# A two-layer hybrid trunk on one core: the tail's products held in traced order on TensorE, and all modulation of the next layer moved beside the tail

## The chip, the cores and the metric

The kernel runs on one core of one Trainium2 chip. The metric is the time of one execution in device microseconds; several executions are timed, and their median is given. TensorE multiplies (PE, with its weight loads as PEld), VectorE (DVE), ScalarE (ACT) and GpSimd (POOL) do the rest, and SyncE (SP) issues the transfers.

## The reference, cut to what matters

Two layers (`DEPTH = 2`), each over 1152 tokens of 1024 channels: 128 context and 1024 latent tokens.

```
def modulation(cvec, mod_w, mod_b):
    m = jax.nn.silu(cvec) @ mod_w + mod_b              # 1024 x 3072, for c and for c_ctx
    return jnp.split(m.reshape(-1, 1, 3 * D_MODEL), 3, axis=-1)
...
    shift, scale, gate = mod
    h = rmsnorm(x, norm_g) * (1 + scale) + shift
    return split_cols(h @ w_in), gate
...
    xb = centred_conv(x_b, P['conv_w'], P['conv_b'])
    ob, st = rglru_bidir(xb, h0, P)                    # gates: two block products per direction
...
    m = jax.nn.sigmoid(merge).reshape(B, T, N_BRANCH, D_MODEL)
    y = (m[:, :, 0] * ((oa * jax.nn.silu(g_a)) @ P['w_br_a'])
         + m[:, :, 1] * ((ob * jax.nn.silu(g_b)) @ P['w_br_b'])
         + m[:, :, 2] * ((oc * jax.nn.silu(g_c)) @ P['w_br_c']))
    return x + gate * (y @ P['w_out'])
```

`merge` is the last 3072 columns of `h @ w_in`. Every product is of float32 operands, cut into a high and a low part and multiplied in three matmuls.

## The kernel before, in words

A layer has three parts. `unit_phase` does the projections and the two attentions. The **tail** does the merge gates and the three branch products. `w_out_phase` does the last projection, in two halves `q` of 512 columns, each 9 token blocks of 24 matmuls of 128x512.

The tail is written as 22 calls of `tail_step` and one of `tail_last`, which has the last two column blocks of branch B. A step has one block of 128 output channels of one branch, in three chunks of 384 tokens. For a chunk, `tail_merge` runs 24 matmuls (`ws_chunk`, over weights `wsh` and `wsl` that are loaded and split for this step) into a PSUM tile `ps_s`, and ACT's Tanh (L1022) takes it to `mg`. `tail_branch` runs 12 matmuls (`oh`, `ol` against `wb`) into `ps_s` or `ps_o`, one chunk later than its merge (three later in two steps), and VectorE multiplies by the gate and adds to `yr`.

Beside the tail runs a generator, `L.rec`, which `tail_step` moves on by one piece a chunk. It first holds the recurrence of branch B, four column blocks of `lru`: the transfer `lx`, one ACT operation into `lu` (L860), nine DVE operations of the convolution on `lu`, the split of `lu` into `luhl` (ACT for the high half, POOL for the low), then 12 groups of three gate matmuls `ps_t<-luhl,gw`, and the scans. Behind these it holds `mod_side`, the **modulation**: pieces of up to 384 columns of `mod_w`, each 1024 rows long, loaded in three parts `modw` (3, 3 and 2 blocks of 128 rows) through two buffers. For each row block and each of two condition vectors one DVE operation multiplies a block into the accumulator `macc` (16 operations a piece). Six matmuls with a column of ones, the **sums** (L957; the hardware runs each in two passes), then add over partitions into `ps_t`, and DVE writes `modt` from it.

Layer 1 has 11 pieces: the three of its own gate, and eight of layer 2. `NMOD = 8` of them run in the tail, the other three in the first half of `w_out_phase`. Layer 2 has none.

A scheduler orders each engine's instructions from its own estimate of durations and from priorities; the order of the program is a wish, data dependencies bind. Tiles come from rings of buffers; a new tile waits until the last reader of the one it replaces is done. The ring `tab` has one buffer, `D` three, `T` two.

Of the kernel before, what the change touches and what calls it, by code (L numbers as in the profile page):

```python
# [2 lines left out]

# [1 line left out]

# [14 lines left out]
NTOK = 1152  # L20
# [6 lines left out]
TPO = 1500  # L27
# [3 lines left out]
NLAG = 3  # L31

LRU0 = 4
NMOD = 8

WUK = 1
XPOS = 1
# [16 lines left out]
def hybrid_dit_kernel(ctx, tc, I, O):  # L54
# [28 lines left out]
    V, A, Pq, T = nc.vector, nc.scalar, nc.gpsimd, nc.tensor  # L83
# [20 lines left out]
    one = tl("one", 1)  # L104
# [61 lines left out]
    def w_in_cols(l, c0):  # L166
        def f(lo):
            dma(lo, I["w_in"][l, :, c0:c0 + 128].rearrange("(k p) n -> p k n", p=128))
        return f

    def mm3(out, lh, ll, rh, rl, first, last):
        T.matmul(out=out, lhsT=r(lh), rhs=r(rh), start=first, stop=False)  # L172
        T.matmul(out=out, lhsT=r(lh), rhs=r(rl), start=False, stop=False)  # L173
        T.matmul(out=out, lhsT=r(ll), rhs=r(rh), start=False, stop=last)  # L174

    class Lay:
        pass
# [662 lines left out]
    def lru(L, ct):  # L840

        l, D = L.l, L.D
# [18 lines left out]
        uhl = {}  # L861
# [15 lines left out]
        for c in range(3):  # L877
            s = slice(384 * c, 384 * c + 384)
            for d in range(2):
                for k, (dst, hb) in enumerate(((ra, D.hba), (ri, D.hbx))):  # L880
                    p = ps("t", 384)
                    m = 2 * k + d
                    mm3(p, wh[:, m, :], wl[:, m, :], uhl[c][:, 0, :], uhl[c][:, 1, :], True, True)
                    A.activation(out=dst[d][:, s], in_=p, func=AF.Tanh, scale=0.5,
                                 bias=hb[:, 4 * d + ct:4 * d + ct + 1])
            if c == 0:
                parts(2)
            yield
            for d in range(2):
                stt(ri[d][:, s], ri[d][:, s], 1.0, u[:, s], ALU.add, ALU.mult)  # L890
# [49 lines left out]
            load_o(L, 1, (k,))  # L940
            yield

    def mod_side(mods, tag, atag):

        seq = [(m, k0, min(k0 + 3, KT)) for m in mods for k0 in range(0, KT, 3)]
        ws = {}

        def load(i):
            (D, b0, n), k0, k1 = seq[i]
            ws[i] = al(tag, "modw", k1 - k0, 128 * n)  # L950
            dma(ws[i], I["mod_w"][D.l, k0 * 128:k1 * 128, b0 * 128:(b0 + n) * 128].rearrange("(k p) n -> p k n", p=128))

        def sums(D, b0, n, acc):
            p = ps("t", n, 2)
            for b in range(n):
                for s in range(2):
                    T.matmul(out=p[:, b, s:s + 1], lhsT=acc[:, s, b * 128:(b + 1) * 128], rhs=one,  # L957
                             start=True, stop=True)
            for s in range(2):
                tt(V, D.modt[:, b0:b0 + n, s], p[:, :, s], D.cols[:, R_MB + b0:R_MB + b0 + n], ALU.add)  # L960
        for i in range(min(2, len(seq))):
            load(i)
        yield
        pend = None
        for i, ((D, b0, n), k0, k1) in enumerate(seq):
            if pend:
                sums(*pend)
                pend = None
            if k0 == 0:
                acc = al(atag, "macc", 2, 128 * n)  # L970
            w = ws.pop(i)
            for k in range(k0, k1):
                for s in range(2):
                    c = sc[:, k, s:s + 1]
                    if k == 0:
                        ts(V, acc[:, s, :], w[:, k - k0, :], c, ALU.mult)
                    else:
                        stt(acc[:, s, :], w[:, k - k0, :], c, acc[:, s, :], ALU.mult, ALU.add)
            if i + 2 < len(seq):
                load(i + 2)  # L980
            if k1 == KT:
                pend = (D, b0, n, acc)
            yield
        if pend:
            sums(*pend)
        yield

    def state_out(L):
# [29 lines left out]
    YSPL = ("PP", "PP", "SS", "SS", "SS", "SS", "SS", "SS")  # L1018

    def tail_merge(L, br, j, c, mw, m):  # L1020
        p = ws_chunk(L, mw[0], mw[1], c)
        A.activation(out=m, in_=p, func=AF.Tanh, scale=0.5)  # L1022

    def tail_branch(L, order, j, c, ohl, wb, m):
        p2 = ps("so"[(j + c) % 2], 384)
        cs = slice(c * 384, (c + 1) * 384)
        for k in range(4):
            mm3(p2, wb[:, 0, k, :], wb[:, 1, k, :], ohl[k][0][:, cs], ohl[k][1][:, cs], k == 0, k == 3)
        yj = L.yr[j][:, cs]
        if order == 0:  # L1030
            stt(yj, m, 1.0, p2, ALU.add, ALU.mult)
        else:
            stt(p2, m, 1.0, p2, ALU.add, ALU.mult)
            tt(V, yj, yj, p2, ALU.add)
        if order < 2:
            if c == 2:
                dma(ysp[j], L.yr[j])
        else:
            y_split(L, j, c)

    def y_tile(L, order, j):

        L.yr[j] = al("tab" if (order, j) == (2, 7) else "Q", "yr", NTOK)
        if order:
            dma(L.yr[j], ysp[j])

# [34 lines left out]
    def tail_last(L, br):  # L1081

        ms = [al("D", "mg2", 2, 384) for _ in range(3)]
        m = lambda j, c: ms[(3 * (j - 6) + c) // 2][:, (3 * (j - 6) + c) % 2, :]
        wbs = {}
        for j in (6, 7):
            mw = ws_load(w_in_cols(L.l, CMG + 1024 * br + 128 * j), KT)
            for c in range(3):
                tail_merge(L, br, j, c, mw, m(j, c))
                if L.late:  # L1090
                    L.late.pop(0)()
        for j in (6, 7):
            wbs[j] = wbr_load(L, br, j)
            y_tile(L, 2, j)
        for c in range(3):
            for j in (6, 7):
                tail_branch(L, 2, j, c, L.o[br], wbs[j], m(j, c))

    def gate_rows(D):

        p = ps("t", 2, 128)
        for s in range(2):
            T.transpose(p[0:8, s, :], D.modt[:, 16:24, s], ident)
        row = al("D", "grow", 2, 128)
        acopy(row[0:8], p[0:8], scale=0.5)
        dma(gbd[D.l], row[0:8])
        grs = []
        for q in range(2):
            gr = al("T", "gr", 2, 512)
            for s in range(2):  # L1110
                dma(gr[:, s, :].rearrange("p (k n) -> p k n", k=4),
                    gbd[D.l, 4 * q:4 * q + 4, s, :][None].to_broadcast([128, 4, 128]))
            grs.append(gr)
        return grs
# [18 lines left out]
    def w_out_phase(L, Ln, grs):  # L1133
        l = L.l
        state_out(L)
        mods = mod_side(L.mods[NMOD:], "Q", "tab")
        wq = [load_wo(L, 0)]
        for q in range(2):
            cs = slice(q * 512, (q + 1) * 512)
# [2 lines left out]
            w, gr = wq[q], grs[q]  # L1142
            last = q == 1 and Ln is not None
            if last:
                for _ in mods:
                    pass
                mod_gs(Ln.D, 0, 8)
                load_unit_consts(Ln)
                alloc_h(Ln, [t for j in range(2, 6) for t in L.y[j]])
            for i in range(9):  # L1150
                if q == 0:
                    next(mods, None)
                    if i == 4 and Ln is not None:
                        Ln.wu = load_wu(Ln, c_groups(0))
                if last and i % 3 < 2:
# [104 lines left out]
    for l in range(DEPTH):  # L1260
        L = Ls[l]
        L.mods = [(L.D, 16, 3), (L.D, 19, 3), (L.D, 22, 2)] if l == 0 else []
        layer_scalars(L.D)
        if l + 1 < DEPTH:
            for _ in layer_vectors(l + 1):
                pass
            Dn = Ls[l + 1].D
            L.mods += [(Dn, b, 3) for b in range(0, 24, 3)]
        unit_phase(L)
        steps = [(2, 0, j) for j in range(8)] + [(0, 1, j) for j in range(8)] + [(1, 2, j) for j in range(6)]  # L1270
        def side():
            L.recd = False
            yield from recurrence(L)
            L.recd = True
            yield from mod_side(L.mods[:NMOD], "T", "tab")
        L.rec = side()
        for n, (br, order, j) in enumerate(steps):
            with tc.high_priority(offset=TPO):
                if n == 0:
                    load_o(L, 2)  # L1280
                    for _ in range(LRU0):
                        next(L.rec, None)
                if n == 7:
                    load_o(L, 0)
                tail_step(L, n, br, order, j, NLAG if n in LAG2 else MLAG)
        with tc.high_priority(offset=TPO):
            for _ in L.rec:
                pass
        grs = gate_rows(L.D)
        tail_last(L, 1)  # L1290
        w_out_phase(L, Ls[l + 1] if l + 1 < DEPTH else None, grs)


# [46 lines left out]
```

## Time and profile before

| | |
|---|---|
| median of 3 runs | 2813.23 us (2809.66 to 2815.37) |
| profiled execution | 2815.96 us, of which the span from first to last instruction is 2813.9 us |
| TensorE busy | 2712.7 us (96%) |
| tail of layer 1 | 802.3 to 1334.0 us |
| w_out of layer 1 | 1334.0 to 1440.8 us, its first half to 1393.2 us |
| tail of layer 2 | 2197.7 to about 2723 us |

Times in the trace are counted from the start of the span. The median is 2.7 us below the profiled execution.

### The profile page before, as it was taken

Reading aid. Unit: us, or ns where it says so; the run is one execution under the profiler, and the core shown is the slowest. Engines: PE = TensorE matmul, PEld = TensorE weight load, DVE = VectorE, ACT = ScalarE, POOL = GpSimd, SP = SyncE. Lnnn points to the kernel's source line nnn. Section 1 sums busy time; section 2 is a strip of 40 time slices with the busy share of each in tenths; the row PEclk is TensorE's granted clock in tenths of the full one; section 3 lists DMA queues with packets and bytes.
Section 4 is the critical chain, followed back from the end, with each engine's and each line's share of the span. In section 5 each row is a group of like instructions: output and inputs, shape, how many; then the busy total and the mean of one; then the engine's idle time right before and its main releaser. Section 6 shows DMA issues by size and latency. Waiting matters only on the chain. (4 is left out here: it accounts for less than half of the span.)

```text
span 2813.9 us, 42868 instructions
## 1 busy us (share of the span) xinstructions
PE 2712.7 (96%) x15821; PEld 2584.6 (92%) x15821; DVE 1702.7 (61%) x4337; ACT 1273.3 (45%) x2536; POOL 1059.8 (38%) x1368
## 2 busy tenths in 40 slices
PE   8999999999999999999999999999999999999999
PEld 4989999999999998999789999999999999999997
DVE  4797778776633556643767887787766244541242
ACT  4465454566634554122143645555666255531210
POOL 1344344451224464122504353545322244542340
PEclk9999999999999999999999999999999999999999
DMA  6010011011222345543630110111112223342232
GB/s 233 26 34 29 24 33 35 25 59 58 87 79 85 105 134 162 184 124 98 193 97 25 34 34 20 34 42 32 53 55 86 88 80 112 127 149 98 78 121 86
DMA packets 230636, 229.32 MB, mean 81 GB/s; under 512 B 21698, under 2 KB 195100, under 8 KB 230428
## 3 DMA queue, kind: packets, MB, share of 16 engines
q1 hardware_dynamic: 230428, 226.60, 25.0%
q8 instruction: 124, 2.03, 0.3%
q14 instruction: 84, 0.69, 0.1%
HBM read 173.32 MB, written 53.24 MB: 81 GB/s over the span
## 5 line engine op out<-in xcount | busy, mean ns | idle before, releaser
L172 PE MATMUL ps_s<-h,wsh 128*128 128x384 f32 x1440 | 492.6, 343 | 16.3 <-ACT mg L1022 13.0
L174 PE MATMUL ps_s<-h,wsl 128*128 128x384 f32 x1440 | 489.8, 341 | 0.0
L173 PE MATMUL ps_s<-h,wsh 128*128 128x384 f32 x1440 | 489.1, 340 | 0.0
L92 POOL TENSOR_TENSOR wsl<-wsraw,wsh 128x256 fp32r<-128x256 f32 x320 | 253.0, 822 | 419.7 <-ACT wsh L89 206.1
L172 PEld LDWEIGHTS ps_s<-h,wsh 128*128 128x128 f32 x1440 | 272.5, 189 | 21.7 <-ACT mg L1022 16.1
L173 PEld LDWEIGHTS ps_s<-h,wsh 128*128 128x128 f32 x1440 | 272.5, 189 | 0.3
L174 PEld LDWEIGHTS ps_s<-h,wsl 128*128 128x128 f32 x1440 | 272.4, 189 | 0.2
L92 POOL TENSOR_TENSOR qkraw<-qkraw,tab 128x384 f32<-128x384 f32 (+2 forms) x92 | 135.2, 1480 | 306.5 <-DVE qkraw L92 168.0
L529 DVE TENSOR_SCALAR_CACHE_REDUCE P<-ps_s 128x384 f32<-128x384 f32 (+1 forms) x400 | 205.0, 538 | 38.5 <-PE ps_s L528 37.4
L172 PE MATMUL ps_s<-uwh,h 128*128 128x384 f32 x648 | 221.6, 344 | 3.1 <-ACT h L89 1.9
L92 DVE TENSOR_TENSOR PT<-ps_t,PT 128x512 fp32r<-128x512 f32 (+2 forms) x304 | 187.4, 625 | 60.5 <-ACT PT L89 59.1
L173 PE MATMUL ps_s<-uwl,h 128*128 128x384 f32 x648 | 219.8, 342 | 0.7 <-POOL uwl L92 0.7
L89 ACT ACTIVATE PT<-ps_t 128x512 fp32r<-128x512 f32 (+2 forms) x304 | 159.4, 545 | 130.9 <-PE ps_o L174 64.5
L174 PE MATMUL ps_s<-uwh,h 128*128 128x384 f32 x648 | 218.2, 344 | 0.0
L539 ACT ACTIVATE P<-P,csm 128x1152 f32<-128x1152 f32 (+1 forms) x144 | 165.8, 1155 | 92.1 <-DVE csm L96 92.1
L92 POOL TENSOR_TENSOR uwl<-wuraw,uwh 128x256 fp32r<-128x256 f32 x192 | 123.0, 674 | 177.2 <-ACT uwh L89 135.1
L1022 ACT ACTIVATE mg<-ps_s 128x384 f32<-128x384 f32 x144 | 69.2, 484 | 264.0 <-DVE ps_o L101 133.2
L172 PE MATMUL ps_s<-yh,wsh 128*128 128x384 f32 x480 | 165.1, 346 | 11.1 <-ACT mg L1022 8.6
L174 PE MATMUL ps_s<-yh,wsl 128*128 128x384 f32 x480 | 163.8, 342 | 0.0
L173 PE MATMUL ps_s<-yl,wsh 128*128 128x384 f32 x480 | 162.7, 340 | 0.0
L92 POOL TENSOR_TENSOR wb<-wbraw,wb 128x256 fp32r<-128x256 f32 x96 | 82.3, 878 | 185.9 <-ACT wb L89 169.0
L101 DVE SCALAR_TENSOR_TENSOR ps_o<-mg,ps_o 128x384 f32<-128x384 f32 x48 | 26.7, 557 | 197.9 <-PE ps_o L174 197.9
(281 smaller groups left out, 7251.5 us busy)
## 6 DMA issues: line engine op xcount, KB each, us to landing
wsraw<-in_w_in_dram SPq DMA_DIRECT2D x80, 512.0 KB, 3.9
ysp<-yr SPq DMA_DIRECT2D x32, 576.0 KB, 5.1
yr<-ysp SPq DMA_DIRECT2D x32, 576.0 KB, 4.1
wuraw<-in_w_in_dram SPq DMA_DIRECT2D x72, 192.0 KB, 3.5
ol<-osp SPq DMA_DIRECT2D x24, 576.0 KB, 5.0
modw<-in_mod_w_dram SPq DMA_DIRECT2D x20, 576.0 KB, 5.0
modw<-in_mod_w_dram SPq DMA_DIRECT2D x16, 512.0 KB, 7.0
woraw<-in_w_out_dram SPq DMA_DIRECT2D x16, 512.0 KB
```

The source lines that it names most:

```text
L89: A.activation(out=out, in_=in_, func=AF.Copy, scale=scale)
L92: e.tensor_tensor(out=out, in0=a, in1=b, op=op)
L101: V.scalar_tensor_tensor(out=out, in0=a, scalar=s, in1=b, op0=op0, op1=op1)
L172: T.matmul(out=out, lhsT=r(lh), rhs=r(rh), start=first, stop=False)
L173: T.matmul(out=out, lhsT=r(lh), rhs=r(rl), start=False, stop=False)
L174: T.matmul(out=out, lhsT=r(ll), rhs=r(rh), start=False, stop=last)
L529: V.tensor_scalar(out=S[:, n * c:n * c + n], in0=p, scalar1=1.0, scalar2=NEG, op0=ALU.mult, op1=ALU.max, accum_out=mx[:, mp, c:c + 1])
L539: A.activation(out=Ss[mp][:, 0:n], in_=Ss[mp][:, 0:n], func=AF.Exp, scale=0.125, bias=nm[:, mp:mp + 1], accum_out=acc)
L1022: A.activation(out=m, in_=p, func=AF.Tanh, scale=0.5)
```

## The change

1. Inside the tail, matmuls get an order among themselves: `mm3` notes its last matmul in `newest`, and `behind()` puts what is issued within it behind that matmul on TensorE. It wraps the merges, the branch products, the gates of `lru` and the sums. It is an order on the engine, not a wait on a semaphore.
2. `NMOD` is gone: all 11 pieces run in the tail's generator. `w_out_phase` has none.
3. The sums of a piece are written two parts of the next piece later (`due`), and the accumulators alternate between the rings `tab` and `D`. The parts `modw` come from `T` throughout.
4. `tail_last` moves the generator on (one piece a chunk beside its first block, two beside its second), then empties it, and calls `gate_rows` (the transposes and broadcasts of the gate, which need the sums) ahead of its last branch products. Before, the generator was emptied and `gate_rows` called ahead of `tail_last`.
5. One `yr` tile moves from ring `tab` to `Q`.

```diff
+    newest = [None]
+    def behind():
+        return tc.issue_after(newest[0].ins) if newest[0] is not None else nullcontext()
...
     def mm3(out, lh, ll, rh, rl, first, last):
         T.matmul(out=out, lhsT=r(lh), rhs=r(rh), start=first, stop=False)
         T.matmul(out=out, lhsT=r(lh), rhs=r(rl), start=False, stop=False)
-        T.matmul(out=out, lhsT=r(ll), rhs=r(rh), start=False, stop=last)
+        newest[0] = T.matmul(out=out, lhsT=r(ll), rhs=r(rh), start=False, stop=last)
...
-                    mm3(p, wh[:, m, :], wl[:, m, :], uhl[c][:, 0, :], uhl[c][:, 1, :], True, True)
+                    with behind():
+                        mm3(p, wh[:, m, :], wl[:, m, :], uhl[c][:, 0, :], uhl[c][:, 1, :], True, True)
...
-            if pend:
-                sums(*pend)
-                pend = None
             if k0 == 0:
-                acc = al(atag, "macc", 2, 128 * n)
+                acc = al(("tab", "D")[i // 3 % 2], "macc", 2, 128 * n)
...
             if k1 == KT:
-                pend = (D, b0, n, acc)
+                due.append((i + 2, (D, b0, n, acc)))
+            if due and due[0][0] == i:
+                sums(*due.pop(0)[1])
             yield
...
                 tail_merge(L, br, j, c, mw, m(j, c))
                 if L.late:
                     L.late.pop(0)()
+                for _ in range(j - 5):
+                    next(L.rec, None)
+        with tc.high_priority(offset=TPO):
+            for _ in L.rec:
+                pass
+        grs = gate_rows(L.D)
...
-        mods = mod_side(L.mods[NMOD:], "Q", "tab")
...
-            yield from mod_side(L.mods[:NMOD], "T", "tab")
+            yield from mod_side(L.mods)
```

The scheduler turns this into other orders, shown here at three places. Numbers behind a name tell one tile of that name from another; after the change the lines of `mm3` are L178 to L180, and the sums L966.

TensorE at the start of layer 1's tail, before: the merge `ps_s_9168` of the second chunk ends and its neighbour's branch product `ps_s_9194` follows.

```order
L173 MATMUL ps_s_9168<-h_310,wsh_9098 128x384
L174 MATMUL ps_s_9168<-h_309,wsl_9099 128x384
L172 MATMUL ps_s_9168<-h_311,wsh_9098 128x384
L173 MATMUL ps_s_9168<-h_312,wsh_9098 128x384
L174 MATMUL ps_s_9168<-h_311,wsl_9099 128x384
L172 MATMUL ps_s_9194<-oh_9037,wb_9107 128x384
L173 MATMUL ps_s_9194<-ol_9038,wb_9107 128x384
L174 MATMUL ps_s_9194<-oh_9037,wb_9107 128x384
L172 MATMUL ps_s_9194<-oh_9046,wb_9107 128x384
```

The same place after: behind the merge `ps_s_9008` stand the gate matmuls of the recurrence's first column block.

```order
L180 MATMUL ps_s_9008<-h_309,wsl_8891 128x384
L178 MATMUL ps_s_9008<-h_311,wsh_8890 128x384
L179 MATMUL ps_s_9008<-h_312,wsh_8890 128x384
L180 MATMUL ps_s_9008<-h_311,wsl_8891 128x384
L178 MATMUL ps_t_9143<-luhl_9085,gw_9068 128x384
L179 MATMUL ps_t_9143<-luhl_9085,gw_9068 128x384
L180 MATMUL ps_t_9143<-luhl_9085,gw_9068 128x384
L178 MATMUL ps_t_9148<-luhl_9085,gw_9068 128x384
L179 MATMUL ps_t_9148<-luhl_9085,gw_9068 128x384
L180 MATMUL ps_t_9148<-luhl_9085,gw_9068 128x384
```

The gates stood 304 matmuls later before. Layer 2 has the same move.

TensorE late in layer 1's tail, before: two branch products run interleaved, and around the transposes of `gate_rows` (L1103) stand the sums of the eighth piece. The sums of the first seven stand ahead of this, each alone between products; those of the last three stand in `w_out_phase`.

```order
L172 MATMUL ps_s_12526<-oh_11374,wb_12257 128x384
L172 MATMUL ps_o_12343<-oh_11374,wb_12081 128x384
L173 MATMUL ps_s_12526<-ol_11375,wb_12257 128x384
L173 MATMUL ps_o_12343<-ol_11375,wb_12081 128x384
L174 MATMUL ps_s_12526<-oh_11374,wb_12257 128x384
L174 MATMUL ps_o_12343<-oh_11374,wb_12081 128x384
L957 MATMUL ps_t_12908<-one_64,macc_12737 128x1
L1103 MATMUL ps_t_13113<-ident_63,modt_91 8x128 x2
L990 MATMUL ps_t_13478<-ident_63,fin_549 8x128
L957 MATMUL ps_t_12908<-one_64,macc_12737 128x1 x5
L172 MATMUL ps_s_12562<-h_297,wsh_12432 128x384
```

After, there is no sum ahead of the last branch product of the 22nd step (`ps_s_13131`); behind it stand those of the first two pieces.

```order
L178 MATMUL ps_s_13131<-oh_11374,wb_12809 128x384
L179 MATMUL ps_s_13131<-ol_11375,wb_12809 128x384
L180 MATMUL ps_s_13131<-oh_11374,wb_12809 128x384
L966 MATMUL ps_t_11711<-one_64,macc_11484 128x1
L966 MATMUL ps_t_11887<-one_64,macc_11651 128x1
L966 MATMUL ps_t_11711<-one_64,macc_11484 128x1
L966 MATMUL ps_t_11887<-one_64,macc_11651 128x1
```

The sums of pieces three and four begin 45 and 110 matmuls behind the last of these, and then, in the middle of `tail_last`, those of the next five stand in a row ahead of the merge `ps_s_13379`.

```order
L179 MATMUL ps_s_13349<-h_312,wsh_13342 128x384
L180 MATMUL ps_s_13349<-h_311,wsl_13343 128x384
L966 MATMUL ps_t_12421<-one_64,macc_12177 128x1 x6
L966 MATMUL ps_t_12605<-one_64,macc_12360 128x1 x6
L966 MATMUL ps_t_12789<-one_64,macc_12543 128x1 x6
L966 MATMUL ps_t_12973<-one_64,macc_12728 128x1 x6
L966 MATMUL ps_t_13157<-one_64,macc_12912 128x1 x6
L178 MATMUL ps_s_13379<-h_297,wsh_13342 128x384
L179 MATMUL ps_s_13379<-h_298,wsh_13342 128x384
```

The sums of pieces ten and eleven begin 45 and 99 matmuls behind these. From the last sum of the second piece to the first matmul of `w_out_phase` it is 308 matmuls, 52 of them sums. In this stretch merges, branch products and sums no longer change places.

VectorE at the same place after: the third accumulator, `macc_11827`, takes the buffer of the first (ring `tab`) and so comes behind the first sums; it stands directly behind the last operation on the 22nd step's branch product.

```order
L100 SCALAR_TENSOR_TENSOR ps_o_13078<-mg_12868,ps_o_13078 128x384
L91 TENSOR_TENSOR yr_12813<-yr_12813,ps_o_13078 128x384
L100 SCALAR_TENSOR_TENSOR ps_s_13131<-mg_12921,ps_s_13131 128x384
L91 TENSOR_TENSOR yr_12813<-yr_12813,ps_s_13131 128x384
L95 TENSOR_SCALAR macc_11827<-modw_11709,sc_83 128x256 x2
L91 TENSOR_TENSOR modt_91<-ps_t_11711,cols_90 128x3 x2
L91 TENSOR_TENSOR modt_91<-ps_t_11887,cols_90 128x3 x2
L100 SCALAR_TENSOR_TENSOR macc_11827<-modw_11709,sc_83,macc_11827 128x256 x4
L100 SCALAR_TENSOR_TENSOR macc_11827<-modw_11783,sc_83,macc_11827 128x256 x6
L100 SCALAR_TENSOR_TENSOR macc_11827<-modw_11834,sc_83,macc_11827 128x256 x4
L95 TENSOR_SCALAR macc_12003<-modw_11885,sc_83 128x384 x2
L100 SCALAR_TENSOR_TENSOR ps_o_13204<-mg_12999,ps_o_13204 128x384
```

The two accumulators ahead of it end 70 instructions earlier; the nine from `macc_11827` on, 144 operations of the modulation, all stand behind it. Before, the accumulators of the first eight pieces were spread between 1082 and 1217 us.

## Rows read from the trace of the kernel before

**Rows 1.** Page, part 1: busy time of each engine, share of the span, instructions.

```profile
PE 2712.7 (96%) x15821; PEld 2584.6 (92%) x15821; DVE 1702.7 (61%) x4337; ACT 1273.3 (45%) x2536; POOL 1059.8 (38%) x1368
```

**Rows 2.** Windows of the two tails and of w_out; columns in the first line.

```profile
core 0: us, PE busy (x) PEld busy (x) DVE busy (x) ACT busy (x) POOL busy (x), PEclk, DMA share, GB/s
802.30:1334.00 531.70, 510.29 (x2859) 504.71 (x2858) 255.87 (x407) 187.54 (x277) 205.34 (x244) 0.98 0.39 125
1334.00:1393.20 59.20, 52.93 (x229) 43.94 (x228) 45.99 (x71) 9.60 (x20) 39.98 (x46) 0.91 0.59 183
1393.20:1440.80 47.60, 47.60 (x224) 39.27 (x223) 26.70 (x68) 14.55 (x42) 0.00 (x0) 1.00 0.46 147
2197.70:2723.00 525.30, 508.68 (x2830) 500.08 (x2829) 197.49 (x278) 189.13 (x279) 216.15 (x259) 0.99 0.33 107
```

**Rows 3.** Waits of TensorE's weight loads, tail of layer 1: total us, times, longest.

```profile
PEld ps_s L172 <- ACT mg L1022: 18.1, 12, 3.5
PEld ps_t L172 <- ACT luhl L89: 3.5, 2, 2.0
PEld ps_o L172 <- DVE yr L92: 2.4, 1, 2.4
PEld ps_s L172 <- ACT wsh L89: 1.8, 1, 1.8
PEld ps_t L173 <- POOL luhl L92: 0.9, 1, 0.9
```

**Rows 4.** The same view, tail of layer 2.

```profile
PEld ps_s L172 <- ACT mg L1022: 12.6, 12, 2.0
PEld ps_o L172 <- DVE yr L92: 3.7, 2, 2.8
...
PEld ps_s L172 <- ACT wsh L89: 1.7, 1, 1.7
```

**Rows 5.** Windows at half clock in w_out and in the second tail.

```profile
1368.58:1378.82 10.24, 8.34 (x26) 7.14 (x27) 10.21 (x21) 1.61 (x5) 5.40 (x7) 0.50 0.71 216
2416.47:2423.30 6.83, 6.22 (x19) 6.22 (x20) 6.62 (x10) 3.57 (x4) 4.95 (x6) 0.50 0.96 305
```

**Rows 6.** Timeline of TensorE in w_out: start, us, engine, operation, idle before it.

```profile
1370.48 0.55 PE L957 MATMUL ps_t<-one,macc 128*128 128x1 f32 x2 [6.27 <-DVE macc L101]
```

**Rows 7.** Timeline, first tail: start, us, engine, line, operation.

```profile
810.98 0.32 SPq L86 DMA_DIRECT2D lx<-xsp  x1
812.26 0.19 PEld L172 LDWEIGHTS ps_s<-oh,wb 128*128 128x128 f32 x1
814.38 0.19 PEld L172 LDWEIGHTS ps_s<-h,wsh 128*128 128x128 f32 x1
```

**Rows 8.** Tile lu, first tail: count, ns min/median/max, first and last start.

```profile
L101 DVE SCALAR_TENSOR_TENSOR lu<-lx,cols,lu x9: 343/744/745, 816.3 to 820.4; 128x512 f32<-128x512 f32 x3, 128x127 f32<-128x127 f32 x2, 128x511 f32<-128x511 f32 x2, 128x126 f32<-128x126 f32 x1
L92 POOL TENSOR_TENSOR luhl<-lu,luhl x4: 455/594/735, 867.6 to 869.4; 128x256 fp32r<-128x256 f32 x2, 128x128 fp32r<-128x128 f32 x2
L89 ACT ACTIVATE luhl<-lu x3: 509/513/514, 865.0 to 868.1; 128x384 fp32r<-128x384 f32 x3
L860 ACT ACTIVATE lu<-lx,cols x1: 1350/1350/1350, 814.9 to 814.9; 128x1152 f32<-128x1152 f32 x1
```

**Rows 9.** Timeline of VectorE, one modulation piece of the first tail.

```profile
1178.81 1.23 DVE L96 TENSOR_SCALAR macc<-modw,sc 128x384 f32<-128x384 f32 x2
1179.95 5.37 DVE L101 SCALAR_TENSOR_TENSOR macc<-modw,sc,macc 128x384 f32<-128x384 f32 x10
1187.63 2.21 DVE L101 SCALAR_TENSOR_TENSOR macc<-modw,sc,macc 128x384 f32<-128x384 f32 x4 [2.31 <-DMA modw<-in_mod_w_dram]
```

**Rows 10.** Tile modw, first tail: from DMA issue to landing.

```profile
DMA to landing us min/median/max: 3.2/4.7/5.2
```

More of the change, by code (lines that the diff above doesn't have):

```diff
@@ L1 @@
 import math
-from contextlib import ExitStack
+from contextlib import ExitStack, nullcontext
 import numpy as np
@@ L33 @@
 LRU0 = 4
-NMOD = 8
 WUK = 1
@@ L941, in recurrence, with mod_side @@
             yield
-    def mod_side(mods, tag, atag):
+    def mod_side(mods):
         seq = [(m, k0, min(k0 + 3, KT)) for m in mods for k0 in range(0, KT, 3)]
-        ws = {}
+        ws, due = {}, []
         def load(i):
             (D, b0, n), k0, k1 = seq[i]
-            ws[i] = al(tag, "modw", k1 - k0, 128 * n)
+            ws[i] = al("T", "modw", k1 - k0, 128 * n)
             dma(ws[i], I["mod_w"][D.l, k0 * 128:k1 * 128, b0 * 128:(b0 + n) * 128].rearrange("(k p) n -> p k n", p=128))
@@ L954, in sums @@
             p = ps("t", n, 2)
[L955 to L958, printed above, removed]
+            with behind():
+                for b in range(n):
+                    for s in range(2):
+                        T.matmul(out=p[:, b, s:s + 1], lhsT=acc[:, s, b * 128:(b + 1) * 128], rhs=one,
+                                 start=True, stop=True)
             for s in range(2):
@@ L963, in mod_side @@
         yield
-        pend = None
         for i, ((D, b0, n), k0, k1) in enumerate(seq):
-            if pend:
-                sums(*pend)
-                pend = None
             if k0 == 0:
-                acc = al(atag, "macc", 2, 128 * n)
+                acc = al(("tab", "D")[i // 3 % 2], "macc", 2, 128 * n)
             w = ws.pop(i)
@@ L981, in mod_side @@
             if k1 == KT:
-                pend = (D, b0, n, acc)
+                due.append((i + 2, (D, b0, n, acc)))
+            if due and due[0][0] == i:
+                sums(*due.pop(0)[1])
             yield
-        if pend:
-            sums(*pend)
+        yield
+        for _, d in due:
+            sums(*d)
         yield
@@ L1020, in tail_merge @@
     def tail_merge(L, br, j, c, mw, m):
-        p = ws_chunk(L, mw[0], mw[1], c)
+        with behind():
+            p = ws_chunk(L, mw[0], mw[1], c)
         A.activation(out=m, in_=p, func=AF.Tanh, scale=0.5)
@@ L1026, in tail_branch @@
         cs = slice(c * 384, (c + 1) * 384)
-        for k in range(4):
-            mm3(p2, wb[:, 0, k, :], wb[:, 1, k, :], ohl[k][0][:, cs], ohl[k][1][:, cs], k == 0, k == 3)
+        with behind():
+            for k in range(4):
+                mm3(p2, wb[:, 0, k, :], wb[:, 1, k, :], ohl[k][0][:, cs], ohl[k][1][:, cs], k == 0, k == 3)
         yj = L.yr[j][:, cs]
@@ L1041, in y_tile @@
     def y_tile(L, order, j):
-        L.yr[j] = al("tab" if (order, j) == (2, 7) else "Q", "yr", NTOK)
+        L.yr[j] = al("Q", "yr", NTOK)
         if order:
@@ L1097, in tail_last @@
                 tail_branch(L, 2, j, c, L.o[br], wbs[j], m(j, c))
+        return grs
     def gate_rows(D):
@@ L1144, in w_out_phase @@
             if last:
-                for _ in mods:
-                    pass
                 mod_gs(Ln.D, 0, 8)
@@ L1151, in w_out_phase @@
                 if q == 0:
-                    next(mods, None)
                     if i == 4 and Ln is not None:
@@ L1269, in hybrid_dit_kernel @@
         unit_phase(L)
+        newest[0] = None
         steps = [(2, 0, j) for j in range(8)] + [(0, 1, j) for j in range(8)] + [(1, 2, j) for j in range(6)]
@@ L1285, in hybrid_dit_kernel @@
                 tail_step(L, n, br, order, j, NLAG if n in LAG2 else MLAG)
[L1286 to L1290, printed above, removed]
+        grs = tail_last(L, 1)
         w_out_phase(L, Ls[l + 1] if l + 1 < DEPTH else None, grs)
```

## The prediction

> **What bounds the kernel now.** I read the page first, then the kernel cut at its stages, then what TensorE waits for in each stage, then single stretches in order of time.
>
> The page says that TensorE is busy for 96% of the span [rows 1], so time can only be won where it waits or runs at half clock, and any wait that is added on it is added to the time. The windows show where [rows 2]: in the tail of layer 1 it is busy 510.3 of 531.7 us, in the first half of w_out 52.9 of 59.2, in the second half all the time. The granted clock (2.4 GHz at 1.00, half of that at 0.50) is 0.98, 0.91 and 1.00 there, and 0.99 in the tail of layer 2.
>
> The waits say what these losses are. In the tail of layer 1 the weight loads wait 26.7 us, of which 18.1 are for `mg` (L1022), the Tanh that empties a merge's PSUM tile [rows 3]: it comes where the scheduler let two products run interleaved, so that both end together and the next finds no free tile. The rest waits for `luhl`, `yr` and `wsh`. Half clock costs 2% of 531.7 us, 10.6, of which part lies in those waits; I take 9. So about 36 us can be had there. Layer 2's waits add up to 22.4, 18.0 [rows 4] and two for `luhl` that read as in layer 1 [rows 3], and one half-clock stretch of 6.83 us costs half of itself, 3.4 [rows 5]: 26 in all. In w_out the first half takes 59.2 us for the same wide matmuls that take 47.6 in the second. One wait is 6.27 us, a sum that stands in TensorE's stream before VectorE has finished its accumulator [rows 6]; about it TensorE is at half clock for 10.24 us [rows 5]. Together with a few sums this is the difference, of which I count 11 as avoidable.
>
> **What the change removes.** Strict order on TensorE ends the interleaving, so the waits for `mg` should go. The weights of a step are then first used a whole merge and branch later than now, and the waits for `wsh` go too. I leave a quarter, 9 us of the 36 in layer 1 and 4 of the 26 in layer 2, for VectorE falling behind while the recurrence ends: **minus 27 and minus 22**. Bounds: all of it goes (minus 36 and 26) or half of it stays (minus 18 and 13). In w_out the sum and its wait are gone and nothing else that waits is put there: **minus 11**. The sums of three pieces, some 4 us, only move from w_out to the tail: nothing in the total. The `yr` tile's other ring I cost at nothing too: its cover are the merges of `tail_last`, and without them it would cost one load, under 5 us.
>
> **What it adds at the start of each tail.** The first column block's gates now stand where the branch product began at 812.26 us [rows 7]. Their data cannot be there. `lx` is issued at 810.98, because its buffer is the one that attention's last product still reads; the order leaves that product directly ahead of the gates, so `lx` can't go sooner. It has landed by 814.9, when ACT starts its 1.35 us on `lu`; the nine DVE operations run from 816.3 to 820.4 plus 0.7, and the split takes 0.51 on ACT and up to 0.73 on POOL [rows 8]. So the gates can start at about 821.7 and have both halves at 822.4: TensorE stands for 9.1 to 10 us. Before, the gates were 304 matmuls later and this chain had other products as cover. Half clock afterwards, as behind the wait in w_out [rows 5, 6], costs 1.7 to 5 more; I take 3. That is **12.5 for each layer, plus 25**. Bounds: 9 and 14 each. For the other three column blocks the order leaves over 260 matmuls between the end of one block's gates and the next one's, at 12 in 2.12 us [rows 7] some 46 us, which covers the 12 us chain above and the scans ahead of it. I cost them at nothing; the bound is the 4.4 us that such waits cost now in each layer [rows 3, 4].
>
> **What it adds at the end of layer 1's tail.** Three queues close into a ring there. TensorE runs no sum ahead of the 22nd step's end. The third accumulator takes the first one's buffer and waits for the first sums. The loads of `modw` for its last part and for all later pieces wait for VectorE, since they have two buffers. So when TensorE reaches the first sums, at a time I call Y, nine of the eleven pieces are still to do, and their sums stand in TensorE's stream ahead of products that need nothing from them: in `tail_last` five in a row. Behind a waiting sum stand the last merges, the last branch products and all of w_out.
>
> How fast do the pieces come? On VectorE one costs 1.23 + 5.37 + 2.21 = 8.8 us, and this one waited 2.31 for a load besides [rows 9]. A part of a piece is issued when the part two before it has been used, takes 4.7 us to land [rows 10], is itself used for 2.9 (a third of 8.8), and some 0.2 pass between: 7.8 us for two parts, 11.7 for a piece of three. So loads, not VectorE, set the pace. The first of the nine has two blocks, its first parts are already there, and it ends at about Y + 8; the eighth after it at Y + 8 + 8 x 11.7 = Y + 101.6. Then follow its sums (1.4 us), the gate transposes and some 30 products, 8.4 in all: w_out begins at Y + 110. Without waits, 256 products at 0.177 and 52 sums would take about 59.7 with the first sums included. The difference is 50; with a little half clock between, **plus 52**. It is 8 times the piece, less 41.4. Bounds: with the shortest landing, 3.2 [rows 10], a piece takes 9.5 and the term is 35; with the longest, 5.2, and VectorE's operations a fifth slower a piece takes 13.3 and it is 65.
>
> VectorE and TensorE wait here on one another; the Trainium skill (TensorE: Matmul & The Clock Gate, "Step-by-step: what each phase is for") says that matmuls stay in program order and only weight loads are pulled ahead. It thus speaks against any product passing a waiting sum; a passing one would make this term nothing and the sum minus 35. The trace bears the rule out: for 6.27 us nothing of w_out passed the sum [rows 6].
>
> Of the loads the trace has 4.7 us [rows 10]. The Trainium skill (DMA: Bandwidth & Descriptors, "Anatomy of one DMA — SWDGE (gpsimd) path") fits a transfer on another issue path as 2.0 us and its bytes at 436 GB/s; an estimate from that page is 3.4 us for 576 KB, which would bring a piece to 9.5 to 10 us and the total to about no change. Here the median of the row decides.
>
> **The sum.** Minus 27, 22 and 11, plus 25 and 52: plus 17 against the profiled execution's 2815.96, so 2833. The median lies 2.7 lower, and the prediction with it: 2830. A difference under 0.2%, 5.6 us, can't be told from none.
>
> **The rivals.**
>
> *Loads land quickly, no change.* With TensorE standing, little else uses the transfer queues, and every load could take 3.2 us instead of 4.7. A piece takes 9.5, the last term is 35, the sum is nothing: 2813. For it speaks the shortest landing [rows 10]; against it that loads took a median of 4.7 while the tail's traffic was far from full, a share of 0.39 [rows 2].
>
> *VectorE sets the pace, faster.* If loads were hidden altogether (parts issued well ahead of their use), a piece would cost VectorE's own 8.8 us, the last term 29, the sum minus 6: 2807. The point from which it decides is 9.5 us for a piece; below it the change gains. For it speaks that pieces now wait little in total; against it that the two buffers allow no more than one part ahead, and that the shown piece waited 2.31 with that [rows 9].
>
> *The order does not hold old waits off, slower still.* Where half of the old waits stay (they were for ACT and VectorE, which have the same work), 18 us of the gain are gone, and with 13 us for a piece the last term is 63, the sum plus 46: 2859.
>
> *The sums bind nothing.* If TensorE on the chip ran another order than the one built, only the removals would remain, minus 60: 2753. In the trace of before TensorE runs the order that was built, so I give this next to nothing.
>
> **How the numbers follow.** The forecast, slower around 2830, has 0.60, and its slow neighbour 0.17. No change within 5.6 us has 0.10, faster 0.13 (VectorE's pace, or old waits going altogether together with a quick piece). The low end of the range, 2807, takes in loads at their quickest; the high end, 2859, half of the old waits and a slow piece. So faster by over 0.2% 0.13, within 0.2% 0.10, slower 0.77. Slower alone lies between 2820 and 2860.
>
> **What would show each step.** In the profile after, the waits for `mg` in both tails should be nearly gone and those for `wsh` too. At the start of each tail TensorE should stand 9 to 10 us before `ps_t<-luhl,gw`, released by ACT's or POOL's `luhl`. Near the end of layer 1's tail, in the last 110 us ahead of w_out, there should be waits of sums for `macc` of some 45 to 50 us, most before the five in a row, with VectorE showing waits for `modw`, and pieces 11 to 12 us apart. The tail of layer 1 should last about 570 us, that of layer 2 about 516, and w_out about 92. The prediction is wrong if the pieces come less than 9.5 us apart, if the gates find their `luhl` ready, or if the waits for `mg` stay.

## The result, and the profile after

The changed kernel takes 2834.88 us (median of 6 runs, 2832.36 to 2842.15) against 2811.95 us (2809.66 to 2815.37) of the kernel before: a ratio of 1.0084, 95% interval 1.0071 to 1.0097. It is 23 us slower. The forecast was 17 us slower.

TensorE does the same work in a longer span, 2833.5 us. Page, part 1, of the changed kernel; its counterpart is [rows 1]:

```profile
PE 2706.1 (96%) x15821; PEld 2584.2 (91%) x15821; DVE 1702.7 (60%) x4337; ACT 1275.4 (45%) x2536; POOL 1059.3 (37%) x1368
```

The windows of the stages, cut at the same places of the program as [rows 2]: tail of layer 1, w_out in its two windows, tail of layer 2. The windows of w_out in [rows 2] end at the 194th and at the 386th of its 432 products, not at the half and the end, so they are cut there too.

```profile
797.30:1378.60 581.30, 524.60 (x2908) 520.82 (x2907) 285.99 (x471) 189.52 (x278) 215.89 (x252) 0.93 0.39 121
1378.60:1422.50 43.90, 43.90 (x194) 36.10 (x193) 16.33 (x21) 8.96 (x19) 27.08 (x38) 1.00 0.68 214
1422.50:1468.70 46.20, 46.20 (x212) 37.94 (x211) 19.96 (x53) 14.57 (x42) 0.00 (x0) 1.00 0.28 94
2222.40:2741.50 519.10, 504.00 (x2829) 499.29 (x2829) 200.77 (x280) 190.10 (x280) 216.66 (x261) 0.99 0.34 108
```

The first tail grew from 531.7 to 581.3 us and its clock fell from 0.98 to 0.93. W_out fell from 106.8 to 90.1, the second tail from 525.3 to 519.1. Cut at equal counts of TensorE's matmuls (a sum counted once), the two profiled spans differ by 19.6 us: the first tail with w_out gives +32.9 (638.5 to 671.4, from the 4576th to the 7820th matmul), the second tail -5.7, the stretches between -2.6, and the part ahead of the first tail -5.0, where nothing was changed. Other profiles reach the first tail between 794 and 800 us, so a few microseconds there mean nothing; I read the stages, not the ends, of single profiles.

What TensorE's weight loads wait for in the first tail (total us, times, longest); compare [rows 3]:

```profile
PEld ps_t L966 <- issue: 35.2, 6, 7.8
PEld ps_o L178 <- DVE yr L91: 10.6, 2, 6.9
PEld ps_t L178 <- ACT luhl L88: 9.3, 1, 9.3
PEld ps_s L180 <- POOL wsl L91: 1.6, 1, 1.6
PEld ps_s L179 <- DVE ol L91: 1.4, 1, 1.4
```

The twelve waits for `mg`, 18.1 us before, and the one for `wsh` are gone. In their place stand the sums (L966), one wait for `luhl`, and `yr`. The new waits in order of time: the gates at the start of the first tail, sums and one branch product late in it, and the gates at the start of the second tail:

```profile
816.36 0.69 PE L178 MATMUL ps_t<-luhl,gw 128*128 128x384 f32 x1 [8.94 <-ACT luhl L88]
...
1298.17 2.73 PE L966 MATMUL ps_t<-one,macc 128*128 128x1 f32 x12 [3.62 <-DVE macc L100]
1308.68 2.73 PE L966 MATMUL ps_t<-one,macc 128*128 128x1 f32 x12 [7.78 <-DVE macc L100]
1318.72 2.73 PE L966 MATMUL ps_t<-one,macc 128*128 128x1 f32 x12 [7.32 <-DVE macc L100]
1329.16 2.73 PE L966 MATMUL ps_t<-one,macc 128*128 128x1 f32 x12 [7.70 <-DVE macc L100]
1339.42 2.73 PE L966 MATMUL ps_t<-one,macc 128*128 128x1 f32 x12 [7.54 <-DVE macc L100]
...
1365.45 0.69 PE L178 MATMUL ps_o<-oh,wb 128*128 128x384 f32 x1 [6.61 <-DVE yr L91]
...
2241.34 0.69 PE L178 MATMUL ps_t<-luhl,gw 128*128 128x384 f32 x1 [8.95 <-ACT luhl L88]
```

The five groups are the five that stand in a row in the built order. Each waits for its accumulator, and they come 10.0 to 10.5 us apart. VectorE's side of the end of the tail (the first operation of the third piece, then of later pieces), with what it waited for in brackets; behind it all that VectorE's `macc` waited for there, and the loads issued there (KB each, median us to landing):

```profile
1266.36 0.62 DVE L95 TENSOR_SCALAR macc<-modw,sc 128x256 f32<-128x256 f32 x2 [1.13 <-PE ps_t L966]
1276.13 0.75 DVE L95 TENSOR_SCALAR macc<-modw,sc 128x384 f32<-128x384 f32 x2 [1.53 <-DMA modw<-in_mod_w_dram]
...
1300.46 0.75 DVE L95 TENSOR_SCALAR macc<-modw,sc 128x384 f32<-128x384 f32 x2 [1.90 <-DMA modw<-in_mod_w_dram]
1306.86 2.21 DVE L100 SCALAR_TENSOR_TENSOR macc<-modw,sc,macc 128x384 f32<-128x384 f32 x4 [0.22 <-DMA modw<-in_mod_w_dram]
1310.59 0.75 DVE L95 TENSOR_SCALAR macc<-modw,sc 128x384 f32<-128x384 f32 x2 [1.53 <-DMA modw<-in_mod_w_dram]
1320.95 0.75 DVE L95 TENSOR_SCALAR macc<-modw,sc 128x384 f32<-128x384 f32 x2 [1.84 <-DMA modw<-in_mod_w_dram]
...
1353.15 1.31 DVE L95 TENSOR_SCALAR macc<-modw,sc 128x384 f32<-128x384 f32 x2 [0.72 <-DMA modw<-in_mod_w_dram]
```

```profile
DVE macc L95 <- DMA modw<-in_mod_w_dram: 11.0, 7, 1.9
DVE macc L100 <- DMA modw<-in_mod_w_dram: 6.6, 8, 1.8
DVE macc L95 <- PE ps_t L966: 1.1, 1, 1.1
```

```profile
modw<-in_mod_w_dram SPq DMA_DIRECT2D x16, 576.0 KB, 4.1
modw<-in_mod_w_dram SPq DMA_DIRECT2D x8, 384.0 KB, 3.3
```

While TensorE stands, a piece begins about every 10.3 us and waits around 2 us for its loads. The trace gives the landing of only four of these loads, but the waits agree: in this stretch the first parts of pieces were issued 3.9 to 4.2 us before the operation that waited for them began. Only the first sums held an accumulator up; after them `macc` waited for loads alone. The window of the five waits of the sums shows what they do to TensorE: busy 13.5 of 46 us, at a granted clock of 0.51, half speed nearly throughout.

```profile
1296.00:1342.00 46.00, 13.50 (x60) 13.31 (x61) 36.53 (x79) 1.75 (x4) 0.00 (x0) 0.51 0.56 156
```

### The profile page after: what moved, and what is told of

Its sections match the earlier page's. It is cut to its first block, busy times and chain, and to the rows that moved or that the text cites. A ratio compares the mean times of both kernels' runs of the same rounds, so it can differ in the third digit from the quotient of the medians.

```text
span 2833.5 us, 42913 instructions
## 1 busy us (share of the span) xinstructions
PE 2706.1 (96%) x15821; PEld 2584.2 (91%) x15821; DVE 1702.7 (60%) x4337; ACT 1275.4 (45%) x2536; POOL 1059.3 (37%) x1368
## 4 chain that ended last, share of the span: by engine, by line
PE 74%; DVE 13%; DMA 5%; ACT 3%; issue 3%; POOL 1%; SPq 1%; ACTq 0%; DVEq 0%; POOLq 0%
PE ps_s L178 18%; PE ps_s L179 18%; PE ps_s L180 18%; PE ps_o L179 2%; PE ps_o L178 2%; PE ps_o L180 2%; DMA modw<-in_mod_w_dram 2%; DVE P L535 2%; PE ps_o L704 2%; PE ps_t L562 2%; PE ps_t L695 1%; PE ps_s L533 1%; PE ps_s L534 1%; DVE macc L100 1%; DVE PT L91 1%
## 5 line engine op out<-in xcount | busy, mean ns | idle before, releaser
L178 PE MATMUL ps_s<-h,wsh 128*128 128x384 f32 x1440 | 493.3, 343 | 2.0 <-ACT wsh L88 1.1
L180 PE MATMUL ps_s<-h,wsl 128*128 128x384 f32 x1440 | 491.3, 341 | 1.3 <-POOL wsl L91 1.3
L178 PEld LDWEIGHTS ps_s<-h,wsh 128*128 128x128 f32 x1440 | 272.6, 189 | 3.9 <-DVE asm L661 2.0
L180 PEld LDWEIGHTS ps_s<-h,wsl 128*128 128x128 f32 x1440 | 272.5, 189 | 1.8 <-POOL wsl L91 1.6
L178 PE MATMUL ps_s<-uwh,h 128*128 128x384 f32 x648 | 221.9, 344 | 3.3 <-ACT h L88 1.9
L180 PE MATMUL ps_s<-uwh,h 128*128 128x384 f32 x648 | 218.3, 344 | 0.0
L180 PE MATMUL ps_s<-yh,wsl 128*128 128x384 f32 x480 | 163.3, 340 | 3.0 <-POOL wsl L91 3.0
L178 PE MATMUL ps_s<-yh,wsh 128*128 128x384 f32 x480 | 164.1, 342 | 1.8 <-DVE asm L661 0.9
L533 PE MATMUL ps_s<-ck,qhl 128*128 128x384 f32 x384 | 134.9, 370 | 5.7 <-DVE P L535 5.4
```

Source lines behind the costliest of these rows:

```text
L180: newest[0] = T.matmul(out=out, lhsT=r(ll), rhs=r(rh), start=False, stop=last)
L533: T.matmul(out=p, lhsT=qh, rhs=kk, start=True, stop=False)
```

## The experiments

Ratios are to the kernel before, run on the same chip beside each; its median was 2806.62 us for e1 to e4, 2806.22 for e5 to e8, 2809.35 for e9 and e10. By its ratio the changed kernel would take about 2830 us there. In e1 to e5 theory A is the prediction's: the change wins by ordering merges and branch products, and loses only by where the gates and the sums stand.

**e1: the sums early.**

```diff
+            with tc.high_priority(offset=3000):
                 with behind():
                     for b in range(n):
                         for s in range(2):
                             T.matmul(out=p[:, b, s:s + 1], ...)
```

> The changed kernel with one edit: the sums get a higher priority in the scheduler, so that they stand in TensorE's stream 109 matmuls apart from the 15th step on, and no longer bunched behind the 22nd. Theory A (the 52 us at the end come from where the sums stand: VectorE waits for TensorE to pass the first sums, then TensorE for VectorE): the wait at the end goes, a piece has 19 us and needs 10 to 12, about 2780 us. Theory B (the modulation is too slow for the tail wherever its sums stand, because of the two load buffers): waits of a few us at each of the 11 sums, 2815 us or more.

Measured 2783.07 us, ratio 0.9921 (0.9904 to 0.9937). The windows of the first tail and of w_out:

```profile
794.30:1319.90 525.60, 508.27 (x2910) 504.69 (x2909) 296.16 (x471) 190.41 (x279) 218.69 (x249) 0.99 0.42 135
1319.90:1409.40 89.50, 89.50 (x403) 73.63 (x402) 36.81 (x74) 22.90 (x60) 30.43 (x41) 1.00 0.45 149
```

No sum waits in this trace, and the first tail is 525.6 us with the same modulation in it: 55.7 under the changed kernel's 581.3 (the timed ratios differ by less, some 46 us). Theory A holds for the largest term. It was a matter of where the sums stand, not of how much modulation the tail can take.

**e2: the gates free.**

```diff
-                    with behind():
-                        mm3(p, wh[:, m, :], wl[:, m, :], uhl[c][:, 0, :], uhl[c][:, 1, :], True, True)
+                    mmg(p, wh[:, m, :], wl[:, m, :], uhl[c][:, 0, :], uhl[c][:, 1, :])
+    def mmg(out, lh, ll, rh, rl):      # mm3 that leaves newest alone
```

> The changed kernel without the fixed order of the recurrence's gates: they stand some 200 matmuls later in the first column block. Theory A (the fixed gates cost 9 to 12 us at the start of each tail): 20 to 24 us less than the changed kernel, less what the kernel before waited at its own gates, 4 us a layer: 2812 to 2820 us. Theory B (fixing the gates costs nothing over the whole tail, because the waits only move to later gates): 2835 us, as the changed kernel.

Measured 2827.66 us, ratio 1.0076 (1.0059 to 1.0092): no difference from the changed kernel that can be told. The waits of the first 240 us of the first tail:

```profile
PEld ps_t L183 <- ACT luhl L88: 8.7, 3, 3.1
PEld ps_s L180 <- POOL wsl L91: 1.8, 2, 1.0
PEld ps_s L179 <- DVE ol L91: 1.7, 1, 1.7
```

The wait of 9.3 us at the first gates is gone, and three of up to 3.1 us at the gates of the other column blocks have come, with half clock behind them (a granted clock of 0.92 to 0.96 in the three stretches named next). Counted by matmuls, 200 of the tail at full speed take 35.3 us; in the free version the stretches from the 5200th to the 5800th take 41.1, 39.9 and 42.7, where the changed kernel has 35.3, 35.3 and 39.3. Theory B was nearer: the fixed order that costs 12 us at the start saves nearly as much later.

**e3: loads once.**

```diff
-            w = ws.pop(i)
+            w = ws[i % 2]                  # the first two parts, for every piece
...
-            if i + 2 < len(seq):
-                load(i + 2)
```

> The changed kernel, but only the first two parts of modw are loaded, and all pieces are computed from these: the loads of the other parts are left out, so the values of the modulation are not the reference's. Theory A (at the end of the tail the loads through two buffers set the pace of a piece, 10.3 us in the changed kernel's trace): a piece falls to VectorE's own 8.8 us, the last eight gain 12 us, about 2823 us. Theory B (VectorE's operations set the pace): 10 us or more a piece, 2833 us.

Measured 2817.91 us, ratio 1.0042 (1.0027 to 1.0057), 12 us under the changed kernel, as theory A has it. The two pieces that start at 1290.47 and 1292.13 are interleaved and done together after 18 us, 9.1 each. But the waits on VectorE say that not all of the rest is the loads:

```profile
DVE xm L91 <- DMA gr<-gbd: 8.9, 1, 8.9
DVE ps_s L100 <- PE ps_s L180: 5.9, 2, 5.3
DVE macc L95 <- PE ps_t L966: 5.5, 3, 2.5
```

No wait for `modw` is left (17.6 us in 15 waits in the changed kernel); waits for sums that free an accumulator, and in w_out one for the gate rows, have come. The scheduler also put the sums of two pieces together here. Cut at counts, the end of the tail from the 7098th to the 7388th matmul fell from 109.6 to 72.7 us, while the stretch up to the 7820th grew from 95.3 to 108.4, as the last pieces now run beside w_out. So e3 shows that the loads set the pace, and its 12 us only roughly what they cost.

**e4: the order alone,** on the kernel before: `behind()` around `tail_merge`'s and `tail_branch`'s products, gates by `mmg`, everything else as it was.

```diff
+        with behind():
+            p = ws_chunk(L, mw[0], mw[1], c)
...
+        with behind():
+            for k in range(4):
+                mm3(p2, wb[:, 0, k, :], wb[:, 1, k, :], ohl[k][0][:, cs], ohl[k][1][:, cs], k == 0, k == 3)
```

> The kernel before with the order of merges and branch products alone; the gates and sums are free, the last three modulation pieces stay in w_out. Theory A (the fixed order of merges and branch products removes the waits for mg and wsh by itself, some 24 us in the first tail and 17 in the second): about 2770 us. Theory B (those waits went because TensorE stood elsewhere, at the gates and the sums, and ACT and VectorE caught up meanwhile): 2795 us or more.

Measured 2785.68 us, ratio 0.9928 (0.9913 to 0.9943): 21 us under the kernel before, between the theories' numbers and nearer to B's. The waits of its second tail:

```profile
PEld ps_t L182 <- ACT luhl L89: 8.7, 3, 3.1
PEld ps_s L179 <- POOL wsl L92: 3.4, 3, 1.9
PEld ps_s L178 <- DVE ol L92: 1.9, 1, 1.9
PEld ps_o L177 <- DVE yr L92: 1.6, 1, 1.6
```

The waits for `mg` and `wsh`, 14.3 us before [rows 4], are gone, while TensorE stands only 4.3 us longer at gates and no longer at sums, which speaks against theory B's cause. But the waits for `luhl` doubled against the 4.4 us of before [rows 3], and those for `ol` and most of those for `wsl` are new: all waits together are 15.6 us, where they were 22.4. So the order does remove the old waits, and new ones took back about half of that.

**e5: three accumulators.**

```diff
-                acc = al(("tab", "D")[i // 3 % 2], "macc", 2, 128 * n)
+                acc = al(("tab", "D", "D")[i // 3 % 3], "macc", 2, 128 * n)
```

> The changed kernel with its accumulators dealt over one buffer of the ring tab and two of D, where it had one of each; sums and gates stand as in the changed kernel, and the sums of the first three pieces come together behind the 22nd step. Theory A (the ring of accumulators is what holds VectorE back until TensorE has passed the first sums): a third piece is done early, eight instead of nine remain, one piece of 10.3 us less at the end: about 10 us under the changed kernel, ratio to before near 1.005. Theory B (VectorE would have been held up anyway, by the loads or its place in the order): the third piece comes no sooner, ratio 1.008 as the changed kernel.

Measured 2829.57 us, ratio 1.0088 (1.0072 to 1.0104); its time can't be told from the changed kernel's, and a gain of 10 us lies outside the interval. The first operations of its third and fourth piece on VectorE:

```profile
1084.90 0.61 DVE L95 TENSOR_SCALAR macc<-modw,sc 128x256 f32<-128x256 f32 x2
1271.98 0.76 DVE L95 TENSOR_SCALAR macc<-modw,sc 128x384 f32<-128x384 f32 x2 [0.20 <-PE ps_t L966]
```

The third piece now comes at 1085 us and the fourth waits for the first sums, where in the changed kernel the third did so (1266.36 us). The ring of accumulators is thus what holds VectorE, as theory A says. The third piece is the small one of two blocks, so the end (from the 7098th to the 7388th matmul) shrinks by 7.2 us only, from 109.6 to 102.4. The time doesn't show these 7 us (0.26%); with intervals of 0.13 to 0.16% on either ratio that is at the edge of what can be told, and it stays open whether something else took them.

**e6: e1 with the gates one step later.**

```diff
-LRU0 = 4
+LRU0 = 0
```

> The kernel with early sums (e1) with LRU0 0 for 4: the recurrence starts one step later in program order, its first gates stand 108 matmuls (19 us) further on, in fixed order as before. Theory A (a fixed gate costs only what its chain lacks in cover, 9 us and the half clock behind it at the start of each tail): both go, 11 us a layer under e1: ratio to before near 0.984, 2762 us. Theory B (the recurrence is a chain through the tail, and what is won at its start is lost at its end, where the next work waits for it): ratio 0.99 or more.

Measured 2772.63 us, ratio 0.9886 (0.9868 to 0.9904), 10 us under e1 and between the theories. The first 224 matmuls of the first tail take 40.9 us (e1: 50.1), of the second (12401st to 12600th) 38.6 (e1: 46.5). But this wait is new, and stands once in each tail:

```profile
PEld ps_s L178 <- ACT oh L88: 5.7, 1, 5.7
```

It is branch B's input, which is loaded when the recurrence is done. The later recurrence gives back 6.1 us in one stretch of the first tail (the 5600th to the 5800th matmul, 45.2 against 39.1) and 4.2 in the second.

**e7: the same by a third less** (`LRU0 = 1`, the edit otherwise that of e6).

> The same with LRU0 1: the first gates stand 72 matmuls (12.7 us) further on than in e1, each group of 12 a chunk apart. Theory A: the cover of 12.7 us is more than the 9 to 10 us that lacked, so the same as e6 within 3 us, ratio near 0.985. Theory B: as e6's, 0.99 or more.

Measured 2777.83 us, ratio 0.9899 (0.9882 to 0.9915). Neither better nor clearly worse than e6: here too the wait for `oh` came, 3.7 us in each tail, and the gates still waited for `luhl`, 2.5 and 2.8 us. The chain itself did not begin later: `lx` was issued 8.7 us into the tail, as in e1, and the convolution was done at 814.74, 4.5 us before TensorE came to the gates. But ACT's split stands behind another operation there, which waited for its own load:

```profile
809.89 4.85 DVE L100 SCALAR_TENSOR_TENSOR lu<-lx,cols,lu 128x126 f32<-128x126 f32 x9 [0.48 <-ACT lu L866]
...
819.93 0.63 ACT L88 ACTIVATE wb<-wbraw 128x512 fp32r<-128x512 f32 x1 [5.57 <-DMA wbraw<-in_w_br_c_dram]
820.47 0.47 ACT L836 ACTIVATE gxt<-ps_s 128x384 f32<-128x384 f32 x1
820.84 0.92 ACT L88 ACTIVATE luhl<-lu 128x384 fp32r<-128x384 f32 x2
```

So theory A's cover was long enough for the chain, and the order on ACT used it up.

**e8: early sums and free gates** (the edits of e1 and e2).

> Early sums as in e1 and free gates as in e2: only merges, branch products and sums in fixed order. Free gates saved 12 us at each tail's start in e2 and gave back 8 to 10 at later gates. Theory A (the give-back belongs to free gates, which float into products and then wait on their own chain): 3 to 5 us under e1, ratio 0.990. Theory B (the give-back came from the other waits of e2): 20 us under e1, ratio 0.985.

Measured 2779.7 us, ratio 0.9907 (0.9892 to 0.9922), as theory A expected. In its first tail the start takes 38.6 us (e1: 50.1) and the stretch from the 4700th to the 7098th matmul 444.1 (e1: 433.3). Free gates give back what they save whatever the sums do.

**e9: later, then caught up.** e6, and

```diff
             next(L.rec, None)
+            if c == 0 and 2 <= n <= 5:
+                next(L.rec, None)
             if c == 1 and not L.recd:
```

> e6 with four more moves of the generator, one each in steps 3 to 6: the first gates stay 108 matmuls further on, from the second column block's end on gates and sums stand where e1 has them. In e6 the start gained 9 us a tail against e1, but 5 us a tail came back as a wait for oh, whose load comes behind the end of the recurrence. Theory A (that give-back belongs to the recurrence's later end alone): the start's gain stays, the wait for oh goes, 17 to 19 us under e1, ratio 0.985 or 0.986. Theory B (any move of the first gates is paid for later in the tail): as e6, 0.989.

Measured 2761.88 us, ratio 0.9833 (0.9818 to 0.9848): 1.7% under the kernel before and the fastest here. The wait for `oh` is gone, the gain at the start stays. The windows of its two tails and of w_out:

```profile
795.30:1314.10 518.80, 509.29 (x2910) 506.38 (x2909) 296.21 (x471) 189.48 (x279) 220.28 (x251) 0.99 0.43 137
1314.10:1403.50 89.40, 89.40 (x402) 73.54 (x400) 37.80 (x74) 22.99 (x59) 28.89 (x39) 1.00 0.46 151
2157.30:2668.00 510.70, 504.58 (x2833) 500.17 (x2832) 203.12 (x282) 189.40 (x280) 218.41 (x261) 1.00 0.34 110
```

**e10: e9 with the modulation divided as before,** the last three pieces in w_out through ring `Q`.

```diff
-            yield from mod_side(L.mods)
+            yield from mod_side(L.mods[:8])
...
+        mods = mod_side(L.mods[8:], "Q", ("tab", "tab"))       # moved on once a block of the first half
```

> e9 with the modulation divided as in the kernel before, eight pieces in the tail and three in w_out's first half; order, gates and sums as in e9. Theory A (moving the last three pieces is worth the stall in w_out, 10 us, whatever else is done): 6 to 10 us over e9, ratio near 0.989. Theory B (the three pieces cost as much in the tail as in w_out): the same as e9 within 3 us.

Measured 2767.89 us, ratio 0.9853 (0.9836 to 0.9869), 6 us over e9, the low end of theory A. The two intervals overlap, but the stages agree: the first tail with w_out, from the 4576th to the 7820th matmul, takes 614.3 us where e9 has 608.2. A sum waits in w_out again:

```profile
PEld ps_t L967 <- issue: 3.0, 1, 3.0
```

So moving the three pieces beside the tail is worth about 6 us, once their sums stand well.

## Why the prediction was right, and where its sizes were off

Cut at equal counts, the terms of the sum can be read one by one from the two traces. The start of the first tail, up to the 4700th matmul, is 12.3 us longer (forecast 12.5); from there to the 7098th, where the first sums stand, it is 24.5 shorter (forecast 27, for the whole tail); the end, to the 7388th, is 56.7 longer (forecast 52); w_out, to the 7820th, is 11.5 shorter (forecast 11). The second tail is 5.7 shorter, where the forecast's minus 22 and plus 12.5 make 9.5. These add up to plus 27, where the sum had plus 17; the time rose by 23.

**What the change removes** was right in kind: no wait for `mg` is left in either tail, and e4 shows that the order alone removes them. In the second tail it gained less than forecast: 520.6 to 514.9 us with the gates' 11.5 in it, so 17 where 22 were forecast. I had left 4 us of waits; the trace has 7.4 without the first gates (3.3 for `wsl`, 1.7 for `yr`, 1.6 for `ol`, 0.8 for `lr` and `li`). In w_out the stall went, and up to the 386th product the stage took 90.1 us where about 92 were forecast.

**The gates** were right to the microsecond: 9.3 us of waiting in each tail, 9.1 to 10 forecast, and 12.3 and 11.5 us with the half clock, 12.5 forecast. What the prediction didn't see is the other side of it. It costed the gates of the other column blocks at nothing and counted their present waits as removed by the order of the merges. e2 and e8 show that the removal hangs on the fixed gates: without them those waits return, larger. Fixing the gates was not a loss of 25 us but about even.

**The end of the first tail** was right in mechanism, and its size came out near by two errors that partly cancel. From the first sums to w_out it took 114.8 us (1263.8 to 1378.6; 110 forecast). While TensorE stood, a piece took 10.3 us and not 11.7, because a load of 576 KB landed in about 4.1 us and one of 384 KB in 3.3, where the trace before has 5.0 and 3.9 (together the 4.7 of [rows 10]). From 1296 to 1342 us no other load was issued, which is what the first rival counted on; that this is the reason was not tested, and the gain was not enough to make that rival come true. But before and behind these waits VectorE has its operations for the tail's products and for `yl` among those of a piece, 1.3 to 4.7 us each, which the prediction left out, and there a piece took 11.5 to 13.8 us. The eight pieces from 1276.13 to 1366.92 took 11.35 us on average, so the last accumulator was done 103.1 us after the first sums, 101.6 forecast. That the mean came so near was luck. From there to w_out it took 11.7 us and not 8.4: the last branch products had waited 6.6 us for `yr`, which stands behind `macc` on VectorE, and began at 1365.45 at half clock. The sums waited 35.2 us and not 45 to 50: pieces came sooner, and at half clock each of the five groups took 2.73 us of that time and not 1.4. That did not slow the pieces, for none of them waited for sums after the first.

The Trainium skill's rule of program order (TensorE: Matmul & The Clock Gate, "Step-by-step: what each phase is for") is borne out again: with tail products behind them whose data were there, TensorE stood up to 7.8 us at one sum.

**The estimate from the page on transfers** (the Trainium skill, DMA: Bandwidth & Descriptors, "Anatomy of one DMA — SWDGE (gpsimd) path"), 3.4 us for 576 KB, was too low for this queue: the changed kernel's trace has 4.1.

That the ring of accumulators starts the chain is shown by e5, that the loads pace it by e3, that it goes with the place of the sums by e1: its stretch from the 7098th to the 7388th matmul takes 53.9 us, against 109.6 in the changed kernel and 52.9 before. Why the scheduler put the sums of two pieces so late although they were traced earlier is not shown by any run. That a higher priority alone moves them points to the priorities, no further.

## What to carry to other kernels

An order without a wait is still a wait, once the ordered instruction lacks its data: everything behind it on that engine inherits it. So for each instruction that is put in a fixed order, count the cover ahead of it in matmuls, and look in the built order where the scheduler has put the small ones: here a priority for 64 one-column matmuls turned a loss of 0.84% into a gain of 0.79%, and moving one group of gates with its catch-up made it 1.67%. And where two engines feed each other through a ring, the bunched place of one side's reads is where the other side stops.

## What the runs showed of the hardware that was not expected

TensorE stood and ran in turns for 46 us at a granted clock of 0.51; in that stretch a group of six sums took 2.73 us, against 1.40 us for the last one, at 1372.01, outside it. A standing TensorE thus pays also for the little that it runs between waits; here VectorE's loads set the pace all the same, so the time did not grow by it. And two profiles of programs that agree up to the first tail reached it 5 us apart (802.3 and 797.3 us), so a difference of 0.2% belongs to the timed ratio and not to one pair of profiles.
